# FFN activations read back later by ScalarE's queue in runs of 32, and state-space products in alternating heads: a two-layer decoder trunk on one Trainium2 core

## The chip, the cores and the metric

The kernel runs on one core of a Trainium2 chip. Five engines work on their own instruction queues: TensorE (PE in the profile, with its weight loads shown apart as PEld), VectorE (DVE), ScalarE (ACT), GpSimd (POOL) and SyncE (SP). A queue is worked off in order, and an instruction that waits for a semaphore holds what stands behind it. SP computes nothing here; it issues the DMAs. The metric is the device time of one execution in microseconds; the median of several runs is compared.

## What is computed

The reference takes 256 tokens of width 2048 through two layers. Cut to what matters here:

```python
for layer in range(2):
    hm = rms_norm(x, g) * (1 + sc_m) + sh_m          # sh, sc, g from the vector c
    y = ab_mixer(hm) if layer == 0 else cd_mixer(hm) # layer 0: gating MLP and a state-space scan
    x = x + (1 + g_m) * y
    hf = rms_norm(x, g) * (1 + sc_f) + sh_f
    x = x + (1 + g_f) * swiglu(hf, w_gate, w_up, w_down)

def swiglu(h, w_gate, w_up, w_down):                 # 2048 -> 5632 -> 2048
    a = silu(h @ w_gate) * (h @ w_up)
    return a @ w_down

def ssd_scan(x, dt, a, b_mat, c_mat):                # 32 heads of 64, chunks of 128 tokens
    ...
    y_diag = einsum('bcgrts,bcsgrp->bctgrp', cb[:, :, :, None] * decay, xc)
    ...
    y_off = einsum('bctgn,bcgrpn,bcgrt->bctgrp', cc, prev, exp(a_cum))
    return y_diag + y_off
```

Everything is float32.

## The kernel before

**Dense products.** A float32 product is made of three products of rounded parts (hi by hi, hi by lo, lo by hi). Weights stream from memory in slabs of two K tiles (128 rows each) by 512 columns. For each slab `wslab` (L322) issues the load on SP (L326, tile `raw`, 4 buffers), a cast on ScalarE (L332, `hi`, 3 buffers) and a rest on VectorE (L337, `lo`, 3 buffers). `dense_as` (L432) then runs the slab's 24 products of 128x512, four column by row groups of three for each tile, through `mm` (L156), with the activations as the stationary operand; `dense_ws` (L384) is the other way around and its products stand at L407. A dense product over 16 K tiles takes 8 slabs. After each slab `dense_as` calls `run_later`, which starts deferred work once DEFER = 6 K tiles of the running product are done, and `pump`, which paces the loads and sums of the modulation weights (`araw`, L234 and L201) beside the dense work.

**Order.** The kernel is written as one list; a planner orders each engine's queue by priority, by what depends on what, and by its own estimate of durations. `tc.high_priority(offset)` moves work ahead; `tc.issue_after` forces one instruction behind another. A deferred piece of work gets the priority of the place where it is called, so a later call means a later priority.

**FFN.** It runs in halves: 6 blocks of 512 columns, then 5, each block a gate product and an up product, and after each half the down product over its 24 or 20 tiles. The first half of layer 0 goes over K in two groups of 8 tiles (`grouped`, L585), with partial sums parked in buffers and put back as a seed (L615). The down product needs the activations transposed (features on partitions), as hi and lo parts. TensorE isn't used for that. `ffn_split` (L1354) calls `turned_by_blocks` (L499) on the block `sg` (silu of gate times up, evicted at L1375 or L1408):

- VectorE transposes 32x32 pieces into a tile `t` (L503, two instructions for each block).
- SP writes `t` to memory as the tensor `flip` with four DMAs (L507).
- A deferred `read` brings it back into `sg`'s own buffer with one DMA of 512 KB on SP (L513, forced behind the latest weight load). It is called when 6 tiles of the next product are done.
- A deferred `use` splits it: ScalarE makes hi (L523), VectorE lo (L524), both over 1024 elements a partition whose source elements lie eight apart. It is called after 10 tiles, or at the end of a product of 8.

This hand-over happens 22 times, 11 in each layer. Tiles of 4 KB a partition come from a pool of 14 buffers (`blk`).

**State-space products.** In layer 0, `ssd_group` (L957) works through four groups of 8 heads, in pairs. For each of the 16 pairs it builds decay masks `m` and `ce` on ScalarE and VectorE, then makes six products into one PSUM tile, head 0 in partitions 0 to 63 (the array's columns 0 to 63), head 1 in 64 to 127. Each is a full float32 product and stands in the trace as two records of 128x128 on 128*64 of the array. They are placed between the slabs of the dense products that run at the time.

Of the kernel before, what the change touches and what calls it, by code (L numbers as in the profile page):

```python
# [15 lines left out]
P = 128  # L16
S = 256
D = 2048
KT = D // P
# [25 lines left out]
F_RATES = (0.8, 0.62)  # L45
R_F1 = 0.5
DEFER = 6
ORDER = ("x4", "v0", "x5", "v1", "x0", "v2", "x1", "v3", "x2", "z0", "x3", "z1", "z2", "z3")
LN_AT = 9
GM_AT = (9, 11, 13, 15)  # L50
# [4 lines left out]
def trunk(ctx: ExitStack, tc: tile.TileContext, x, c, norm_mix_g, norm_ffn_g, ada_w, ada_b,  # L55
# [3 lines left out]
    nc = tc.nc  # L59
    V, A, G, T = nc.vector, nc.scalar, nc.gpsimd, nc.tensor  # L60
# [30 lines left out]
    def pm():  # L91
        return psM.tile([P, 512], F32, tag="m", name="pm")
# [62 lines left out]
    def mm(o, a, b, first=True, last=True):  # L155
        return T.matmul(o, a, b, start=first, stop=last, skip_group_check=True)  # L156
# [114 lines left out]
    wlast = [None, None]  # L271
# [76 lines left out]
    later = deque()  # L348
    dense_mm = [None]
    behind = [None]  # L350

    def run_later(done):
        while later and done >= (later[0][0] if isinstance(later[0], tuple) else 0):
            f = later.popleft()
            (f[1] if isinstance(f, tuple) else f)()

    preps = deque()

# [25 lines left out]
    def dense_ws(w, c0, ks, ahead=W_AHEAD, into=None, seeded=False, begun=None, ends=None):  # L384

        acc = (into or acc_tile()).rearrange("p (n t) -> p n t", n=4)
        done = 0
        for run in slabs(ks):  # L390
            run_prep()
            hi, lo = wslab(w, run[0][0], len(run), c0, 512, ahead)
            if ends and run[-1] is ks[-1]:
                ends()
            ops = []
            for i, (_, (bh, bl)) in enumerate(run):
                done += 1
                ops += [(hi[:, i, :], bh, done == 1, False), (hi[:, i, :], bl, False, False),
                        (lo[:, i, :], bh, False, done == len(ks))]
            if done <= 2:  # L400
                order = [(n, o) for i in (0, 2, 1) for n in range(4) for o in ops[i:i + 1]] \
                    + [(n, o) for n in range(4) for o in ops[3:]]
            else:
                order = [(n, o) for i in range(0, len(ops), 3) for n in range(4) for o in ops[i:i + 3]]
            for n, (a, b, first, final) in order:
                with (tc.issue_after(turned_sums[0].ins) if ends and done == len(ks) else ExitStack()):
                    dense_mm[0] = T.matmul(acc[:, n, :], a[:, n * P:(n + 1) * P], b,  # L407
                                           start=first and n % 2 == 0 and not seeded, stop=final, skip_group_check=True)
                if done == len(ks):
                    ends = None  # L410
            if begun and done == len(run):
                begun()
            if done >= min(DEFER, len(ks)):
                run_later(done if done < len(ks) else KT)
            pump()
        return acc

# [14 lines left out]
    def dense_as(w, c0, ks, ahead=W_AHEAD, head=None, tail=False, hold=False, into=None, seeded=False,  # L432
                 begun=None):

        if tail:
            accs = [pm(), pm()]
        else:
            full = (into or acc_tile()).rearrange("p (n t) -> p n t", n=2)  # L440
            accs = [full[:, 0, :], full[:, 1, :]]
        runs = list(slabs(ks))
        parts = [runs[:2]] if head else []
        end = len(runs) - 3 * tail
        parts += [[r] for r in runs[2 * len(parts):end]] + ([runs[end:]] if tail else [])
        done = 0
        for pi, part in enumerate(parts):
            begin = head and pi == 0
            made = []
            for j, run in enumerate(part):  # L450
                if not begin:
                    run_prep()
                made.append((run, *(ready.popleft() if ready else wslab(w, run[0][0], len(run), c0, 512, ahead))))
            done += sum(len(run) for run in part)
            ops = [(r, i, x) for r in range(len(part)) for x in range(3) for i in range(len(part[r]))]
            if begin:
                ops = [(r, i, x) for xs in ((0, 2), (1,)) for r in range(len(part)) for i in range(len(part[r]))
                       for x in xs]
            if len(part) > 1:
                order = [(n, j, o) for n in range(2) for j, o in enumerate(ops)]  # L460
            else:
                order = [(n, j, o) for j, o in enumerate(ops) for n in range(2)]
            for n, j, (r, i, x) in order:
                if begin and (n, j) in ((0, 0), (0, len(ops) - 2)):
                    head(int(j > 0))
                if begin and n == 1 and j == 8:
                    run_prep()
                run, hi, lo = made[r]
                bh, bl = run[i][1]() if callable(run[i][1]) else run[i][1]

                def product(n=n, j=j, i=i, x=x, bh=bh, bl=bl, hi=hi, lo=lo, last=pi == len(parts) - 1):
                    return mm(accs[n], (bl if x == 1 else bh)[:, n * P:(n + 1) * P], (lo if x == 2 else hi)[:, i, :],
                              first=pi == 0 and j == 0 and not seeded, last=last and j == len(ops) - 1)

                if hold and len(part) > 1 and n == 1 and j >= len(ops) - 2:
                    held.append(product)
                    continue
                with (tc.issue_after(dense_mm[0].ins) if len(part) > 1 and n == 1 and j == 0 else ExitStack()):
                    dense_mm[0] = product()
            if begun and pi == 0:  # L480
                begun()
            if done >= min(DEFER, len(ks)):
                run_later(done if done < len(ks) else KT)
            for _ in part:
                if not (tail and done > len(ks) - 16):
                    pump()
        return accs if tail else full
# [11 lines left out]
    def turned_by_blocks(src):  # L499

        t = bt()
        for cc in range(2):
            V.transpose(t.rearrange("p (c j f k) -> p k f c j", c=4, f=4, k=2)[:, cc],  # L503
                        src[:, cc, :].rearrange("p (f c j) -> p f c j", f=4, c=4))
        d = dram.tile([4, 32, 4, S], F32, tag="flip", name="flip", bufs=3)
        for q in range(4):
            nc.sync.dma_start(d[:, :, q, :].rearrange("c i x -> i c x"),  # L507
                              t[32 * q:32 * q + 32, :].rearrange("i (c x) -> i c x", c=4))
        back = src.rearrange("p c n -> p (c n)")

        def read():
            with tc.issue_after(wlast[0].ins):
                nc.sync.dma_start(back, d.rearrange("c i q x -> (c i) (q x)"))  # L513

        later.append(read)
        return back.rearrange("p (t m) -> p m t", m=8)

    def hslot(k):
        return (hp.tile([P, S], F32R, tag="h%d" % k, name="h%d" % k),
# [2 lines left out]
    def split(dst, src):  # L522
        A.activation(dst[0], src, AF.Copy)  # L523
        V.tensor_tensor(dst[1], src, dst[0].bitcast(F32), op=OP.subtract)  # L524
# [141 lines left out]
    with tc.high_priority(offset=50000):  # L666
# [25 lines left out]
        for k in range(0, KT, 2):  # L692
            ps = pm()
            for j in range(2):
                for cc in range(2):
                    src = xtok[2 * cc + (k + j) // 8][:, ((k + j) % 8) * P:((k + j) % 8 + 1) * P]
                    o = j * S + cc * P
                    last = mm(ps[:, o:o + P], src, diag[:, cc * P:(cc + 1) * P], first=(j == 0 and cc == 0))
# [258 lines left out]
    def ssd_group(g):  # L957
# [11 lines left out]
        xc = []  # L969
# [17 lines left out]
        for j in range(4):  # L987
# [14 lines left out]
            decay(kt + 2)  # L1002
            V.tensor_tensor(cev, cev, cT[:, None, P:S].to_broadcast([P, 2, P]), op=OP.mult)
            py = pm()
            for i in range(2):
                o = py[i * 64:(i + 1) * 64]
                es = slice((2 * j + i) * 64, (2 * j + i + 1) * 64)
                mm(o[:, 0:P], xc[0][:, es], m[:, i * S:i * S + P])
                mm(o[:, P:S], xc[1][:, es], m[:, i * S + P:(i + 1) * S], first=False, last=False)
                mm(o[:, P:S], sta[:, es], ce[:, i * P:(i + 1) * P], first=False)  # L1010
            V.scalar_tensor_tensor(xtile(kt), xtile(kt), dcol[:, kt:kt + 1], py[:, 0:S], op0=OP.mult, op1=OP.add)

    sums = st([P, 2, 4], "sums")
# [340 lines left out]
    def ffn_split(sg, f, a):  # L1354
        back, made = turned_by_blocks(sg), []

        def use():
            made.extend([b4(F32R), b4(F32R)])
            split([t.rearrange("p n (c t) -> p (n c) t", c=2) for t in made], back)

        later.append((DEFER + 4, use))
        for n in range(4):
            a.append((f + n, lambda n=n: [t[:, n, :] for t in made]))

# [246 lines left out]
```

## Time and profile before

| | |
|---|---|
| median of 3 runs | 2549.71 us (2549.46 to 2554.17) |
| the profiled execution | 2552.85 us, its span 2551.1 us |
| granted TensorE clock, mean | 0.998 |
| chain that ended last, by engine | PE 88%, DMA 5%, DVE 3%, ACT 2% |
| DMA queue of SP | 696.93 MB, 81.2% of the 16 engines' span |
| DMA queue of ScalarE | two small loads at the start |

The page gives for each engine its busy time and count of instructions, and for groups of like instructions the line in the kernel, the engine, what is written from what, the shape and count, then the busy time and mean duration, then the idle time of the engine just before them and who ended it. TensorE's matmuls are pipelined: the record of one 128x512 product lasts 0.39 us, but in a full stream one starts every 0.23 us, so lost time is read from how many start in a stretch, not from the busy share. A row of the table of stretches has the stretch, its length, the busy time and count of the engine asked for, the granted clock, the share of the DMA engines and GB/s. A row of the timeline has the start, the duration, engine, line, operation, tiles, shape and count, and in brackets the idle time before and its releaser.

### The profile page before, as it was taken

To read this page: it belongs to the slowest core of one execution; us is meant where nothing else is said; L and a number is where in the kernel's file an instruction comes from. 1 tells how busy PE (TensorE), PEld (TensorE's weight loads), DVE (VectorE), ACT (ScalarE), POOL (GpSimd) and SP (SyncE) were. 2 spreads that over 40 slices of the span, in tenths; PEclk is the share of its full clock that TensorE was granted. 3 is DMA by queue.
4 is the path that set the end of the run, shared out by engine and by line. 5 is a ranking of instruction groups with operands and counts; after the bars stand their busy time and mean duration, and the time that the engine had idled before them with its cause. 6 is when DMAs were issued, how large, how long until landed. Compare 5 with 4: busy or idle time off the path is not lost.

```text
span 2551.1 us, 33276 instructions
## 1 busy us (share of the span) xinstructions
PE 2512.1 (98%) x12293; PEld 2105.1 (83%) x12293; DVE 1881.4 (74%) x1983; ACT 1329.0 (52%) x1670; POOL 5.0 (0%) x19
## 2 busy tenths in 40 slices
PE   7999999999999999999999999999999999999999
PEld 6989898878788778888888788888788888888887
DVE  7888888899778788777888777667775555555554
ACT  5566876455645554334444665545744444344443
POOL 0000000000000000000000000000000000000000
PEclk9999999999999999999999999999999999999999
DMA  9998668989799899998999688888686776666665
GB/s 339 320 357 312 195 213 274 312 306 305 257 328 335 302 335 364 321 312 318 339 333 324 216 292 256 272 262 278 200 286 221 223 222 206 202 210 212 218 221 166
DMA packets 325533, 699.07 MB, mean 274 GB/s; under 512 B 26096, under 2 KB 39930, under 8 KB 325370
## 3 DMA queue, kind: packets, MB, share of 16 engines
q1 hardware_dynamic: 325242, 696.93, 81.2%
q8 instruction: 96, 1.57, 0.2%
q14 instruction: 67, 0.55, 0.1%
q10 hardware_dynamic: 128, 0.02, 0.0%
HBM read 683.15 MB, written 13.70 MB: 273 GB/s over the span
## 4 chain that ended last, share of the span: by engine, by line
PE 88%; DMA 5%; DVE 3%; ACT 2%; issue 2%; SPq 1%; DVEq 0%; ACTq 0%
PE accps L156 73%; PE accps L407 8%; PE pm L156 6%; DMA blk<-flip 1%; DMA flip<-blk 1%; PE pm L153 1%; DVE acc L201 1%; DVE lo L337 1%; ACT blk L523 1%; ACT hi L332 1%; DMA raw<-in_ffn_w_gate 0%; SPq L507 0%; DMA blk<-in_ada_w 0%; DVE blk L503 0%; DMA raw<-in_ffn_w_down 0%
## 5 line engine op out<-in xcount | busy, mean ns | idle before, releaser
L332 ACT ACTIVATE hi<-raw 128x1024 fp32r<-128x1024 f32 (+1 forms) x864 | 898.5, 1045 | 1032.2 <-PE accps L156 816.5
L337 DVE TENSOR_TENSOR lo<-raw,hi 128x1024 fp32r<-128x1024 f32 (+1 forms) x864 | 1035.7, 1206 | 467.2 <-ACT hi L332 460.5
L156 PE MATMUL accps<-hi,h 128*128 128x512 f32 x2224 | 603.8, 392 | 6.3 <-ACT hi L332 6.3
L156 PE MATMUL accps<-lo,h 128*128 128x512 f32 x2224 | 602.2, 392 | 1.4 <-DVE lo L337 1.2
L156 PE MATMUL accps<-hi,l 128*128 128x512 f32 x2224 | 601.4, 391 | 0.0
L156 PEld LDWEIGHTS accps<-lo,h 128*128 128x128 f32 x2224 | 415.8, 188 | 92.0 <-DVE lo L337 5.7
L156 PEld LDWEIGHTS accps<-hi,l 128*128 128x128 f32 x2224 | 417.3, 188 | 87.6 <-issue 0.8
L156 PEld LDWEIGHTS accps<-hi,h 128*128 128x128 f32 x2224 | 413.1, 188 | 92.6 <-ACT hi L332 8.9
L201 DVE SCALAR_TENSOR_TENSOR acc<-araw,ct,acc 128x1024 f32<-128x1024 f32 (+2 forms) x377 | 465.6, 1235 | 4.2 <-DMA araw<-in_ada_w 3.4
L156 PE MATMUL accps<-hi,blk 128*128 128x512 f32 x1440 | 357.2, 390 | 0.0
L156 PEld LDWEIGHTS accps<-hi,blk 128*128 128x128 f32 x1440 | 269.7, 188 | 56.2 <-ACT hi L332 0.3
L156 PE MATMUL accps<-lo,blk 128*128 128x512 f32 x720 | 192.9, 390 | 1.0 <-DVE lo L337 1.0
L407 PE MATMUL accps<-h,hi 128*128 128x256 f32 x624 | 163.3, 285 | 2.2 <-ACT hi L332 1.4
L407 PE MATMUL accps<-h,lo 128*128 128x256 f32 x624 | 164.4, 287 | 0.9 <-DVE lo L337 0.9
L407 PE MATMUL accps<-l,hi 128*128 128x256 f32 x624 | 162.5, 285 | 1.2 <-DVE l L567 1.2
L156 PEld LDWEIGHTS accps<-lo,blk 128*128 128x128 f32 x720 | 135.0, 188 | 29.7 <-DVE lo L337 1.8
L407 PEld LDWEIGHTS accps<-h,hi 128*128 128x128 f32 x624 | 114.4, 192 | 4.3 <-ACT hi L332 1.6
L407 PEld LDWEIGHTS accps<-h,lo 128*128 128x128 f32 x624 | 114.1, 193 | 2.7 <-DVE lo L337 1.7
L407 PEld LDWEIGHTS accps<-l,hi 128*128 128x128 f32 x624 | 114.2, 193 | 1.6 <-DVE l L567 1.4
L524 DVE TENSOR_TENSOR blk<-blk 128x1024 fp32r<-128x1024 f32 x22 | 47.7, 2168 | 79.2 <-ACT blk L523 79.2
L523 ACT ACTIVATE blk<-blk 128x1024 fp32r<-128x1024 f32 x22 | 47.4, 2157 | 73.1 <-DMA blk<-flip 72.9
L156 PE MATMUL pm<-hi,blk 128*128 128x512 f32 x224 | 57.1, 391 | 0.0
(281 smaller groups left out, 1361.3 us busy)
## 6 DMA issues: line engine op xcount, KB each, us to landing
araw<-in_ada_w SPq DMA_DIRECT2D x323, 512.0 KB, 5.7
raw<-in_ffn_w_gate SPq DMA_DIRECT2D x176, 512.0 KB, 4.9
raw<-in_ffn_w_up SPq DMA_DIRECT2D x176, 512.0 KB, 5.1
raw<-in_ffn_w_down SPq DMA_DIRECT2D x176, 512.0 KB, 4.8
raw<-in_ab_w_in SPq DMA_DIRECT2D x128, 512.0 KB, 4.9
raw<-in_cd_w_in SPq DMA_DIRECT2D x96, 512.0 KB, 4.6
raw<-in_ab_w_out SPq DMA_DIRECT2D x64, 512.0 KB, 5.5
raw<-in_cd_w_out SPq DMA_DIRECT2D x32, 512.0 KB, 5.1
```

Source lines behind the costliest of these rows:

```text
L153: return T.transpose(dst, src, ident)
L156: return T.matmul(o, a, b, start=first, stop=last, skip_group_check=True)
L201: V.scalar_tensor_tensor(acc, r, ct[nr][:, g:g + 1], acc, op0=OP.mult, op1=OP.add)
L332: A.activation(hi, raw, AF.Copy)
L337: wlast[1] = V.tensor_tensor(lo, raw, hi.bitcast(F32), op=OP.subtract)
L407: dense_mm[0] = T.matmul(acc[:, n, :], a[:, n * P:(n + 1) * P], b, start=first and n % 2 == 0 and not seeded, stop=final, skip_group_check ...
L523: A.activation(dst[0], src, AF.Copy)
L524: V.tensor_tensor(dst[1], src, dst[0].bitcast(F32), op=OP.subtract)
```

## The change

Three edits. In the hand-over, the transposes write another layout, in which the 32 elements that one split instruction reads in turn lie side by side; the read-back is issued by ScalarE's queue and no longer forced behind a weight load; the read is called 10 K tiles after the hand-over and the split 14, counted over all dense products in `run_later` by a running count, no longer within the next product. In the state-space products the two heads of a pair alternate.

```diff
+FLIP_READ = 10
+FLIP_SPLIT = 14
...
-    def run_later(done):
-        while later and done >= (later[0][0] if isinstance(later[0], tuple) else 0):
-            f = later.popleft()
-            (f[1] if isinstance(f, tuple) else f)()
+    timed = []
+    ktiles = [0]
+
+    def after_tiles(n, f):
+        timed.append((ktiles[0] + n, len(timed), f))
+        timed.sort(key=lambda e: e[:2])
+
+    def run_later(now, n):
+        ktiles[0] += n
+        while timed and timed[0][0] <= ktiles[0]:
+            timed.pop(0)[2]()
+        while later and now:
+            later.popleft()()
...
-            if done >= min(DEFER, len(ks)):
-                run_later(done if done < len(ks) else KT)
+            run_later(done >= min(DEFER, len(ks)), len(run))
...
-            V.transpose(t.rearrange("p (c j f k) -> p k f c j", c=4, f=4, k=2)[:, cc],
+            V.transpose(t.rearrange("p (c f k j) -> p k f c j", c=4, f=4, k=2)[:, cc],
                         src[:, cc, :].rearrange("p (f c j) -> p f c j", f=4, c=4))
...
-        def read():
-            with tc.issue_after(wlast[0].ins):
-                nc.sync.dma_start(back, d.rearrange("c i q x -> (c i) (q x)"))
-
-        later.append(read)
-        return back.rearrange("p (t m) -> p m t", m=8)
+        after_tiles(FLIP_READ, lambda: nc.scalar.dma_start(back, d.rearrange("c i q x -> (c i) (q x)")))
+        return back.rearrange("p (q m i) -> p m q i", q=4, i=32)
...
+            os = [py[i * 64:(i + 1) * 64] for i in range(2)]
+            es = [slice((2 * j + i) * 64, (2 * j + i + 1) * 64) for i in range(2)]
             for i in range(2):
-                o = py[i * 64:(i + 1) * 64]
-                es = slice((2 * j + i) * 64, (2 * j + i + 1) * 64)
-                mm(o[:, 0:P], xc[0][:, es], m[:, i * S:i * S + P])
-                mm(o[:, P:S], xc[1][:, es], m[:, i * S + P:(i + 1) * S], first=False, last=False)
-                mm(o[:, P:S], sta[:, es], ce[:, i * P:(i + 1) * P], first=False)
+                mm(os[i][:, 0:P], xc[0][:, es[i]], m[:, i * S:i * S + P])
+            for i in range(2):
+                mm(os[i][:, P:S], xc[1][:, es[i]], m[:, i * S + P:(i + 1) * S], first=False, last=False)
+            for i in range(2):
+                mm(os[i][:, P:S], sta[:, es[i]], ce[:, i * P:(i + 1) * P], first=False)
...
-            split([t.rearrange("p n (c t) -> p (n c) t", c=2) for t in made], back)
-
-        later.append((DEFER + 4, use))
+            split([t.rearrange("p n (c q i) -> p (n c) q i", c=2, q=4) for t in made], back)
+
+        after_tiles(FLIP_SPLIT, use)
```

`dense_ws` calls `run_later` in the same new way. The layout of `flip` in memory and the four writes on SP stay as they were.

More of the change, by code (lines that the diff above doesn't have):

```diff
@@ L481, in dense_as @@
                 begun()
-            if done >= min(DEFER, len(ks)):
-                run_later(done if done < len(ks) else KT)
+            run_later(done >= min(DEFER, len(ks)), sum(len(run) for run in part))
             for _ in part:
```

## The prediction

> **What bounds the kernel now.** I read the page first (busy time, then the costliest groups), next a table of stretches, then the waits, and last the timeline around two hand-overs of the turned FFN activations.
>
> ```profile
> PE 2512.1 (98%) x12293; PEld 2105.1 (83%) x12293; DVE 1881.4 (74%) x1983; ACT 1329.0 (52%) x1670; POOL 5.0 (0%) x19
> ...
> L332 ACT ACTIVATE hi<-raw 128x1024 fp32r<-128x1024 f32 (+1 forms) x864 | 898.5, 1045 | 1032.2 <-PE accps L156 816.5
> L337 DVE TENSOR_TENSOR lo<-raw,hi 128x1024 fp32r<-128x1024 f32 (+1 forms) x864 | 1035.7, 1206 | 467.2 <-ACT hi L332 460.5
> ...
> L524 DVE TENSOR_TENSOR blk<-blk 128x1024 fp32r<-128x1024 f32 x22 | 47.7, 2168 | 79.2 <-ACT blk L523 79.2
> L523 ACT ACTIVATE blk<-blk 128x1024 fp32r<-128x1024 f32 x22 | 47.4, 2157 | 73.1 <-DMA blk<-flip 72.9
> ```
>
> TensorE is the bound: 98% busy. ScalarE's weight casts (L332) wait for TensorE to free a buffer, 816.5 us in all, so they are early. What is not TensorE's own pace can only be won in small holes. The 22 splits of turned activations (L523, L524) take twice the time of a weight cast or rest of the same 1024 elements, 2157 against 1045 ns and 2168 against 1206, and ScalarE stands 72.9 us waiting for their data. How many of these microseconds reach TensorE, the stretches tell.
>
> ```profile
> 1010.00:1130.00 120.00, 120.00 (x531) 1.00 0.94 326
> 840.00:960.00 120.00, 115.04 (x498) 0.99 0.94 320
> 1150.00:1160.00 10.00, 8.98 (x38) 1.00 0.72 254
> 1240.00:1250.00 10.00, 9.26 (x39) 1.00 0.70 248
> ```
>
> An undisturbed stretch of 120 us holds 531 products, so one takes 0.226 us. The second K group of layer 0's first FFN half (840 to 960) holds 33 fewer: 33 x 0.226 = **7.5 us** lost. Ten undisturbed microseconds hold 44.2; 1150 to 1160 and 1240 to 1250 miss 6.2 and 5.2: **2.6 us** at two hand-overs of the later half. For layer 1 I take the waits, between 1860 and 2460 us for the weight load, and over the whole run for the DMA queue:
>
> ```profile
> PEld accps L156 <- DVE lo L337: 2.8, 5, 0.7
> ```
>
> ```profile
> SPq L513 <- DMA flip<-blk: 70.6, 38, 4.4
> ```
>
> So layer 1 loses at most **2.8 us**, and SP, which issues every weight load, stands 70.6 us in front of the read-back (L513) until the flip's writes have landed. What that does is seen at the second hand-over, first on SP, then on the engines:
>
> ```profile
> 872.55 0.39 SPq L326 DMA_DIRECT2D raw<-in_ffn_w_gate  x1
> 877.18 0.34 SPq L513 DMA_DIRECT2D blk<-flip  x1
> 877.57 0.43 SPq L326 DMA_DIRECT2D raw<-in_ffn_w_gate  x1
> ```
>
> ```profile
> 882.89 2.04 ACT L523 ACTIVATE blk<-blk 128x1024 fp32r<-128x1024 f32 x1 [5.04 <-DMA blk<-flip]
> 884.84 1.99 ACT L332 ACTIVATE hi<-raw 128x1024 fp32r<-128x1024 f32 x2
> 884.96 2.08 DVE L524 TENSOR_TENSOR blk<-blk 128x1024 fp32r<-128x1024 f32 x1 [5.86 <-ACT blk L523]
> 885.93 0.19 PEld L156 LDWEIGHTS accps<-hi,h 128*128 128x128 f32 x1 [3.51 <-ACT hi L332]
> ```
>
> SP issues nothing from 872.94 to 877.18: 4.2 us. The read lands 5.7 us after its issue, ScalarE stands 5.04 us before the split and works 2.04 on it, and two casts follow only at 884.84. TensorE's weight load has by then waited 3.51 us. In layer 1 the same pattern is milder:
>
> ```profile
> 2268.27 1.06 ACT L332 ACTIVATE hi<-raw 128x1024 fp32r<-128x1024 f32 x1 [1.66 <-PE accps L156]
> 2270.99 1.06 ACT L332 ACTIVATE hi<-raw 128x1024 fp32r<-128x1024 f32 x1 [1.66 <-PE accps L156]
> 2276.45 2.15 ACT L523 ACTIVATE blk<-blk 128x1024 fp32r<-128x1024 f32 x1 [4.40 <-DMA blk<-flip]
> 2278.51 1.05 ACT L332 ACTIVATE hi<-raw 128x1024 fp32r<-128x1024 f32 x1
> ```
>
> ```profile
> 2280.72 4.63 DVE L337 TENSOR_TENSOR lo<-raw,hi 128x1024 fp32r<-128x1024 f32 x4
> 2280.76 1.07 PE L156 MATMUL accps<-hi,l 128*128 128x512 f32 x4
> 2282.00 0.77 PEld L156 LDWEIGHTS accps<-lo,h 128*128 128x128 f32 x4 [0.59 <-DVE lo L337]
> ```
>
> Casts come every 2.72 us (2268.27, 2270.99), one for each slab of two K tiles; with three buffers a cast serves a slab three later, so ScalarE may be late by 3 x 2.72 - 1.06 = 7.1 us. The cast due at 2273.71 starts at 2278.51, 4.8 late, inside that. But VectorE's rests start behind its own 2.17 us split and miss TensorE by 0.59 us.
>
> **The change part by part. Split (14 tiles, runs of 32).** The elements now lie 32 side by side, no longer eight apart, which is the layout of the weight cast. ScalarE's split falls from 2.16 to about 1.05 us, VectorE's from 2.17 to 1.21. That is 2.1 us sooner for the rests behind them; layer 1's holes are 0.7 us or less. The transposes that write this layout:
>
> ```profile
> L503 DVE STREAM_TRANSPOSE blk<-blk 128x512 f32<-128x512 f32 x44 | 47.4, 1159 | 0.0
> ```
>
> No row shows one writing runs of 32. From 1159 (nothing won) down to half of it, 0.58 us, by the ratio 2157 to 1045; I take 0.6, because the strided write is their only oddity. The flip's writes then leave about 1.1 us earlier. All this is ScalarE and VectorE time beside TensorE, worth only what the holes hold.
>
> **Read-back on ScalarE's queue (10 tiles).** SP loses 22 issues of 0.34 us and 70.6 us of standing; the weight loads behind it go out on time. ScalarE gains 22 issues, for which there is one row:
>
> ```profile
> 0.80 0.98 ACTq L113 DMA_DIRECT2D t<-in_c  x2
> ```
>
> 0.49 us each, 10.8 us together, hidden because the casts are early (above); without that cover it would be 10.8 us. ScalarE also gains the wait for the flip's writes. Behind it on that engine stand the weight casts, then SiLU and the seeding copies; VectorE's rests and TensorE wait for those casts. Ten tiles are 5 x 2.72 = 13.6 us after a product ends. In layer 1 the eviction of the product begins at 2261.02 and SP saw the writes landed at 2272.81, 11.8 us later, 10.7 with faster transposes: a read standing at its own position waits for nothing. The planner may put it earlier, as it did the old split, which stands before the cast of 2273.71 though written after 10 tiles. Between nothing and SP's 4.4 us, I take 2 to 3 us: one cast late, inside the 7.1. The read still lands 3.6 (layer 1) to 5.7 us after issue; the split follows two slabs, 5.4 us, later. Its wait shrinks from 4.4 to at most 2 us, and what is late next is nothing that TensorE asks for.
>
> So: layer 1 wins **2.0** of 2.8; the later half of layer 0 **2.4** of 2.6. Of the 7.5 us in 840 to 960 I take **4.5**: the transfers there run at 320 GB/s with a share of 0.94, against 326 in the undisturbed stretch, so part of the hole is the DMA engines' own limit and stays. The bounds are 0 and 7.5. The last block of each five-block half is needed by TensorE at tile 16 of the down projection, one slab (2.72 us) after the split's position; the split takes 1.05 + 1.21 = 2.3. Were it late, that costs up to 3 us at two places; I put it at nothing and leave it to the range. Buffers: the turned tile lives four tiles longer, the split's pair is taken four tiles later, and the next hand-over is 16 tiles off.
>
> The DMA page speaks against the queue change. The Trainium skill, "DMA: Bandwidth & Descriptors", section "Issuing engines are not separate DMA queues", says that DMAs from scalar, sync and gpsimd share the same 16 engines and that issuing on several saves only the sequencer's time to initiate. By that alone SP would be spared 22 x 0.34 us, all hidden, and the three terms would be nothing (first rival). The rows of SP show what it does not count: 70.6 us in which the issuing sequencer stands and the weight loads behind it aren't issued.
>
> **State-space products.** Each pair of heads makes six products, each two records. The records of a head fill one half of the array's columns (128*64).
>
> ```profile
> 367.86:368.87 1.01, 1.01 (x9) 1.00 0.65 156
> ...
> 564.58:565.16 0.58, 0.58 (x5) 1.00 0.90 307
> 566.05:568.16 2.11, 2.11 (x29) 1.00 1.02 310
> 572.71:573.78 1.07, 1.07 (x13) 1.00 0.95 314
> sum 17.22, PE 17.22; mean PE 1.15
> ```
>
> ```profile
> 374.80 0.27 PE L156 MATMUL pm<-t,sta 128*64 128x128 f32 x1
> 374.86 0.27 PE L156 MATMUL pm<-t,xc 128*64 128x128 f32 x1
> 374.91 0.27 PE L156 MATMUL pm<-t,sta 128*64 128x128 f32 x1
> 374.97 0.27 PE L156 MATMUL pm<-t,xc 128*64 128x128 f32 x1
> ```
>
> These are fifteen runs, first and last with the sum (each count holds one record of what follows). Eight records of one half in 1.01 us and four in 0.58: 0.108 us each and 0.15 for entering and leaving the mode. Where records of both halves alternate, as at 374.80, one starts every 0.056 us: two run at once. Today they overlap only in the middle of a run, since a head's three products come first; a run of twelve takes 1.07. Fully paired it takes 0.15 + 12 x 0.054 = 0.80, and all 192 take 15 x 0.15 + 192 x 0.054 = 12.6 instead of 17.2: **4.6 us** at best, nothing at worst. VectorE is the next limit there:
>
> ```profile
> 515.00:580.00 65.00, 65.00 (x340) 51.38 (x339) 61.84 (x77) 36.49 (x69) 3.45 (x6) 1.00 0.87 298
> ```
>
> 61.84 of 65 us busy; half of the saving falls into this stretch, which could shrink to 62.7 and VectorE would be full. I take **3.5**.
>
> **Sum:** 3.5 + 2.0 + 2.4 + 4.5 = 12.4 us. The profiled execution took 2552.85 us (its span is 2551.1, 1.75 lie around it) and would take 2540.4; it stands 3.1 over the median 2549.71, from which I get **2537**.
>
> **Rivals.** (1) *The wait only changes its queue* (the page's rule): ScalarE stands where SP stood, and the casts come as late as today. For it: the read cannot start before the writes land. Against it: the weight loads are freed and the split is halved. The flip terms are nothing, 2549.7 - 3.5 = 2546. Chance 0.17. (2) *The pairing gives nothing*, because VectorE or a planner's new order takes it back: 2549.7 - 8.9 = 2541. For it, 61.84 of 65; against it, the 0.056. Chance 0.15. (3) *Slower:* no cast stands between read and split in ScalarE's queue. At the second hand-over it would stand 4.2 us for the writes, 0.5 issuing, 5.7 for the read, 1.05 on the split: 11.5. The cast due 2.72 us into that is 8.8 late, 1.7 over the 7.1; with the rest's 1.2 behind it up to 2.9. Eleven such hand-overs in layer 0 are 19 to 32 us, in place of the 10.1 lost today, less 5.5 won elsewhere: +4 to +16, about 2560. It decides from 7.1 us of lateness on; one cast between (5.8 + 5.7 standing, the next cast 6 late) avoids it. Chance 0.10, since the two are written two slabs apart.
>
> **How the numbers follow.** Forecast 0.58. The range reaches from all bounds won (4.6 + 2.8 + 2.6 + 7.5 = 17.5: 2532, and 3 for a shifted order) to rival 1 with both late splits and some noise: 2529 to 2551; outside are rival 3 and a tail, under 0.2. A change of 0.2% is 5.1 us, about what a measurement can tell from none. Faster: 0.58, rival 2's 0.13 and a little of rival 1: 0.74. Same: 0.16. Slower: 0.10.
>
> **What would show it.** Right: no SP wait at the read; splits of about 1.05 and 1.21 us; transposes near 0.6; about 525 products or more in 840 to 960; the fifteen runs near 12.6 us in sum, a lone run of twelve at 0.8. Wrong: weight loads of TensorE waiting for casts behind an ACT wait on the flip's writes; VectorE filling the state-space stretch; 0.108 between records there.

## The result, and the profile after

The changed kernel takes 2538.58 us (median of 4 runs, 2536.96 to 2539.53), the kernel before beside it 2549.59: a ratio of 0.9947, with an interval of 0.9935 to 0.996. The profiled execution took 2539.53 us, its span is 2537.8. It is faster by 11 us; 2537 was predicted. The sum came out; one of its largest terms had the wrong cause, as the experiments show.

The page of the changed kernel, then one row of its table of groups and two of its DMA issues (name, queue, count, KB each, median us from issue to landing):

```profile
PE 2502.1 (99%) x12293; PEld 2097.3 (83%) x12293; DVE 1843.9 (73%) x1983; ACT 1302.9 (51%) x1670; POOL 5.0 (0%) x19
...
L528 DVE TENSOR_TENSOR blk<-blk 128x1024 fp32r<-128x1024 f32 x22 | 26.9, 1224 | 48.3 <-ACT blk L527 48.3
L527 ACT ACTIVATE blk<-blk 128x1024 fp32r<-128x1024 f32 x22 | 23.3, 1059 | 68.2 <-DMA blk<-flip 68.2
```

```profile
L512 DVE STREAM_TRANSPOSE blk<-blk 128x512 f32<-128x512 f32 x44 | 28.6, 688 | 0.0
```

```profile
flip<-blk SPq DMA_DIRECT2D x88, 128.0 KB, 4.4
blk<-flip ACTq DMA_DIRECT2D x22, 512.0 KB, 5.1
```

Each operation became as cheap as foreseen: splits of 1.06 and 1.22 us, transposes of 0.69 in place of 1.16. But ScalarE still stands 68.2 us in front of the split, against 72.9 before. The waits of ScalarE and of SP's queue:

```profile
ACT blk L527 <- DMA blk<-flip: 68.2, 20, 5.1
ACT hi L334 <- DMA flip<-blk: 20.2, 6, 5.1
```

```profile
SPq L328 <- DMA flip<-blk: 4.0, 5, 1.2
```

SP's 70.6 us in front of the read are gone, and ScalarE has taken over at least 20.2 of them. The stretches of the prediction (time, PE, PEld, DVE, ACT and POOL busy with counts, clock, DMA share, GB/s):

```profile
840.00:960.00 120.00, 116.30 (x512) 94.00 (x510) 94.26 (x90) 59.67 (x61) 0.00 (x0) 1.00 0.94 334
1150.00:1160.00 10.00, 10.00 (x45) 8.27 (x45) 9.22 (x8) 3.65 (x4) 0.00 (x0) 1.00 1.02 382
1240.00:1250.00 10.00, 10.00 (x45) 8.26 (x45) 7.72 (x8) 4.25 (x4) 0.00 (x0) 1.00 1.01 377
```

The two hand-overs of layer 0's later half have no hole any more. The second K group holds 512 products, against 498 before and 531 undisturbed: 19 are still lost, 4.3 us. (A second profile of the same kernel, c_after_again below, has 525 there.) Rows of the second hand-over, from three views of the engines:

```profile
862.85 2.94 ACT L334 ACTIVATE hi<-raw 128x1024 fp32r<-128x1024 f32 x3
...
872.21 0.33 ACTq L519 DMA_DIRECT2D blk<-flip  x1
872.91 1.06 ACT L334 ACTIVATE hi<-raw 128x1024 fp32r<-128x1024 f32 x1 [7.12 <-PE accps L158]
874.02 0.76 PEld L158 LDWEIGHTS accps<-hi,h 128*128 128x128 f32 x4 [1.57 <-ACT hi L334]
...
878.98 1.06 ACT L527 ACTIVATE blk<-blk 128x1024 fp32r<-128x1024 f32 x1 [2.06 <-DMA blk<-flip]
881.04 0.77 PEld L158 LDWEIGHTS accps<-hi,h 128*128 128x128 f32 x4 [1.46 <-ACT hi L334]
```

```profile
869.99 0.54 SPq L236 DMA_DIRECT2D araw<-in_ada_w  x1
875.25 0.37 SPq L328 DMA_DIRECT2D raw<-in_ffn_w_gate  x1
```

ScalarE ends three casts at 865.79 and then stands until the read leaves at 872.21; the cast behind it starts at 872.91 and TensorE's weight load has waited 1.57 us for it. (The view puts the 7.12 us down to a product, the last of several releasers. The order of the queue shows that the read, which waits for the flip's writes, stood ahead.) ScalarE stands again before the split, and TensorE waits another 1.46 us. SP isn't free either: between 870.53 and 875.25 it issues nothing. Its waits between 866 and 890 us:

```profile
SPq L328 <- DVE lo L339: 11.7, 5, 4.6
```

A load of weights needs a buffer that the rest (L339) of an earlier slab has read, and the rest follows the late cast.

### The profile page after: what moved, and what is told of

Its sections match the earlier page's. It is cut to its first block, busy times and chain, and to the rows that moved or that the text cites. A ratio compares the mean times of both kernels' runs of the same rounds, so it can differ in the third digit from the quotient of the medians.

```text
span 2537.8 us, 33322 instructions
## 1 busy us (share of the span) xinstructions
PE 2502.1 (99%) x12293; PEld 2097.3 (83%) x12293; DVE 1843.9 (73%) x1983; ACT 1302.9 (51%) x1670; POOL 5.0 (0%) x19
## 3 DMA queue, kind: packets, MB, share of 16 engines
q8 instruction: 96, 1.57, 0.2%
## 4 chain that ended last, share of the span: by engine, by line
PE 90%; DMA 4%; DVE 3%; ACT 2%; issue 1%; SPq 0%; DVEq 0%; ACTq 0%
PE accps L158 76%; PE accps L418 7%; PE pm L158 6%; DVE acc L203 1%; PE pm L155 1%; DMA blk<-flip 1%; DMA raw<-in_ffn_w_down 1%; DMA flip<-blk 1%; DVE lo L339 1%; ACT hi L334 0%; DMA araw<-in_ada_w 0%; DMA blk<-in_ada_w 0%; DVE t L957 0%; ACT t L1031 0%; DMA raw<-in_ffn_w_gate 0%
## 5 line engine op out<-in xcount | busy, mean ns | idle before, releaser
L339 DVE TENSOR_TENSOR lo<-raw,hi 128x1024 fp32r<-128x1024 f32 (+1 forms) x864 | 1034.8, 1204 | 518.8 <-ACT hi L334 513.3
L418 PEld LDWEIGHTS accps<-h,hi 128*128 128x128 f32 x624 | 113.9, 191 | 4.0 <-ACT hi L334 1.6
L418 PEld LDWEIGHTS accps<-h,lo 128*128 128x128 f32 x624 | 113.3, 191 | 3.4 <-DVE lo L339 2.3
L418 PEld LDWEIGHTS accps<-l,hi 128*128 128x128 f32 x624 | 113.3, 191 | 1.9 <-DVE l L571 1.4
L528 DVE TENSOR_TENSOR blk<-blk 128x1024 fp32r<-128x1024 f32 x22 | 26.9, 1224 | 48.3 <-ACT blk L527 48.3
L527 ACT ACTIVATE blk<-blk 128x1024 fp32r<-128x1024 f32 x22 | 23.3, 1059 | 68.2 <-DMA blk<-flip 68.2
```

The costliest lines, as they stand in the source:

```text
L339: wlast[1] = V.tensor_tensor(lo, raw, hi.bitcast(F32), op=OP.subtract)
```

## The experiments

In this table the stand of ScalarE is the sum of its waits for the flip's writes and for the read, and of its 22 splits. Waits that the view puts down to another releaser, like the 7.12 us above, are missing from it. Like the second group it is read from the one profiled execution, and not from the median beside it. The second group is the time from the first transposes of hand-over 1 to those of hand-over 6, both in layer 0, in each profile; the same kernel gave 120.4 and 117.9, and 113.3 and 112.2, so differences under 3 us say little.

| kernel | layout, read's queue, heads | median us | ratio, interval | ScalarE, us | second group, us |
|---|---|---|---|---|---|
| before | old, SP, apart | 2549.59 | 1 | 72.9 + 47.4 = 120 | 123.5 |
| e1_pairs_only | old, SP, alternating | 2550.37 | 0.9991, 0.9982 to 1.0 | 73.4 + 47.4 = 121 | 122.4 |
| e8_fast_transpose | transposes new, SP, apart | 2544.9 | 0.997, 0.9961 to 0.998 | 60.1 + 47.5 = 108 | 118.2 |
| e9_fast_split | split new, SP, apart | 2542.97 | 0.9961, 0.9949 to 0.9973 | 72.3 + 23.3 = 96 | 117.3 |
| e3_layout_only | new, SP, apart | 2539.16 | 0.9944, 0.9932 to 0.9957 | 63.6 + 23.3 = 87 | 114.0 |
| e4_old_layout | old, ScalarE, alternating | 2564.26 | 1.0046, 1.0034 to 1.0058 | 47.7 + 59.4 + 47.4 = 155 | 127.8 |
| e2_handover_only | new, ScalarE, apart | 2540.41 | 0.9954, 0.9941 to 0.9966 | 24.9 + 65.8 + 23.3 = 114 | 119.6 |
| after | new, ScalarE, alternating | 2538.58 | 0.9947, 0.9935 to 0.996 | 20.2 + 68.2 + 23.3 = 112 | 120.4 |
| c_after_again | the same | 2540.35 | 0.9949, 0.9937 to 0.9962 | 26.1 + 67.2 + 23.3 = 117 | 117.9 |
| e7_pool_queue | new, GpSimd, alternating | 2540.81 | 0.9957, 0.9944 to 0.997 | 85.7 + 23.3 = 109 | 117.6 |
| e10_later_read | new, ScalarE later, alternating | 2533.78 | 0.993, 0.9918 to 0.9943 | 10.6 + 47.7 + 23.3 = 82 | 113.9 |
| e5_sync_queue | new, SP, alternating | 2535.15 | 0.9927, 0.9915 to 0.994 | 59.7 + 23.3 = 83 | 113.3 |
| e5_again | the same | 2534.94 | 0.9933, 0.9919 to 0.9946 | 59.7 + 23.3 = 83 | 112.2 |

The ratios are each to the kernel before on the same chip, whose median lay between 2549.59 and 2553.35.

**The heads alone, and the hand-over alone.** e1 takes only the alternating products into the kernel before; e2 is the changed kernel with them put back:

```
...
             for i in range(2):
...
-                mm(o[:, 0:P], xc[0][:, es], m[:, i * S:i * S + P])
-                mm(o[:, P:S], xc[1][:, es], m[:, i * S + P:(i + 1) * S], first=False, last=False)
-                mm(o[:, P:S], sta[:, es], ce[:, i * P:(i + 1) * P], first=False)
+                mm(os[i][:, 0:P], xc[0][:, es[i]], m[:, i * S:i * S + P])
+            for i in range(2):
+                mm(os[i][:, P:S], xc[1][:, es[i]], m[:, i * S + P:(i + 1) * S], first=False, last=False)
+            for i in range(2):
+                mm(os[i][:, P:S], sta[:, es[i]], ce[:, i * P:(i + 1) * P], first=False)
```

> The kernel before with the alternating heads alone; the hand-over is untouched. Theory (the two edits are independent and TensorE takes the whole of what the pairing frees): the fifteen or so runs of state-space records cost about 13.0 us in sum in place of 17.2, and the kernel is 4.2 us shorter, ratio 0.9984. Rival (VectorE, 61.84 of 65 us busy there, takes it back): the runs cost 13.0 but the first hand-over starts less than 2 us earlier than before and the ratio is over 0.9992.

> The changed kernel with the heads of a pair one after the other again. Theory (independent edits): the hand-overs bring 9 us of span whatever comes before them: 3 in the second K group of layer 0, 3 in layer 0's later half, 2.5 in layer 1; ratio 0.9965. Rival (the hand-over's gain is partly a shift of the plan by the earlier state-space work): under 6 us and another share by stage.

e2 gives 0.9954, a larger gain than the 0.9965 of its theory; by stage its profile shows 3.9, 2.5 and 1.8 us, for the 3, 3 and 2.5 foreseen. e1 gives 0.9991, between the two theories, with an interval that reaches 0.2% of gain and none. Together they make 0.55%, the whole change 0.51 to 0.53%: the two edits add up as far as the runs can tell. The profiled execution of e1, 2544.33 us, is the fastest of its 11, and that of e2, 2545.94 us, the slowest of its 5, so their stages stand for one execution and not for the median. The state-space records themselves are plain. Three of the 17 stretches of the changed kernel that hold all 192, first, a lone run of twelve and last, and the sum of all 17:

```profile
367.05:368.07 1.02, 1.02 (x17) 1.00 0.63 173
...
563.06:563.87 0.81, 0.81 (x14) 1.00 0.88 341
567.94:568.75 0.81, 0.81 (x14) 1.00 0.97 283
sum 13.05, PE 13.05; mean PE 0.77
```

They took 17.2 us and take 13.05. A run of twelve takes 0.81 (the counts include neighbours), as foreseen. In wall time the medians give 2.5 us (before to e1), 1.8 (e2 to after, on two chips) and 4.0 (e3 to e5_sync_queue, which also differ in where the read and the split are called).

**The layout alone.** e3 is the kernel before with only the three views changed, the read on SP at its old place:

```
-            V.transpose(t.rearrange("p (c j f k) -> p k f c j", c=4, f=4, k=2)[:, cc],
+            V.transpose(t.rearrange("p (c f k j) -> p k f c j", c=4, f=4, k=2)[:, cc],
...
-        return back.rearrange("p (t m) -> p m t", m=8)
+        return back.rearrange("p (q m i) -> p m q i", q=4, i=32)
...
-            split([t.rearrange("p n (c t) -> p (n c) t", c=2) for t in made], back)
+            split([t.rearrange("p n (c q i) -> p (n c) q i", c=2, q=4) for t in made], back)
```

> The kernel before with the runs of 32 alone (transposes, split); the read stays on SP, forced behind a weight load and called at 6 tiles. Theory (the split and the rests behind it were layer 1's and the later half's holes, the queue was the hole of the second K group): layer 1 wins its 2.4 us, the later half of layer 0 most of its 3, the second K group 1 or less because SP still stands 3 to 4 us before the read; ratio 0.9978, about 5.5 us. Rival (the queue is what counts): under 2 us in all, TensorE still waits for rests and casts at the layer 1 hand-overs.

Both theories missed. The layout alone brings 0.56%, some 14 us, as much as the whole change, with the order of instructions on TensorE, ScalarE, SP and GpSimd unchanged. Its second K group, and its SP queue:

```profile
840.00:960.00 120.00, 119.90 (x534) 98.97 (x533) 100.74 (x96) 63.25 (x63) 0.00 (x0) 1.00 0.98 349
```

```profile
SPq L513 <- DMA flip<-blk: 69.8, 42, 5.2
```

SP stands in front of the read as long as before, 69.8 against 70.6 us, and TensorE loses nothing in that group. So SP's standing alone doesn't make the hole, nor does the DMA engines' rate: they now move 349 GB/s there.

**Which half of the layout.** e8 has only the new transposes, e9 only the new split (the first pair of lines of the diff above, or the other two). Each alone hands the features to the down product in another order, so these two don't compute the reference; the instructions and their order on every engine are those of the kernel before.

> The kernel before with the new transposes (runs of 32 written side by side) and the old strided split, so that the features meet the down product in another order. Theory S (the split's 1.1 us less on ScalarE and 0.95 less on VectorE, right ahead of weight casts, are the gain): the transposes alone are worth little, ratio 0.998 to 1.0. Theory W (the transposes, 0.45 us each and ahead of the writes, let writes, read and split all come earlier): ratio 0.9945 to 0.996.

> The kernel before with the old strided transposes and the new split over runs of 32, the features again in another order. Theory S: nearly all of the layout's gain, ratio 0.9945 to 0.996, with the transposes still at 1.16 us and the splits at 1.06 and 1.22. Theory W: ratio 0.998 to 1.0.

Both halves count, and neither theory was right alone: 0.997 and 0.9961. Their second groups, e8 and e9:

```profile
840.00:960.00 120.00, 118.03 (x520) 96.04 (x519) 100.91 (x92) 66.43 (x61) 0.00 (x0) 1.00 0.95 338
```

```profile
840.00:960.00 120.00, 118.94 (x524) 96.67 (x523) 101.44 (x92) 61.59 (x62) 0.00 (x0) 1.00 0.97 339
```

498 products became 520 with the transposes, 524 with the split, 534 with both. Two transposes before the writes are 0.94 us shorter (2 x (1159 - 688)), the split 1.1 on ScalarE: about 2 us of one serial chain, transposes, writes, read, split, then the cast for which TensorE waits. At the second hand-over this chain, from the start of the transposes to the start of the cast behind the split, takes 17.9 us before, 16.3 in e8, 17.2 in e9 and 15.5 in e3.

**The read's queue alone.** e5 is the changed kernel with the read issued by SP; on ScalarE nothing else moves, and the orders of TensorE and VectorE stay the same:

```
-        after_tiles(FLIP_READ, lambda: nc.scalar.dma_start(back, d.rearrange("c i q x -> (c i) (q x)")))
+        after_tiles(FLIP_READ, lambda: nc.sync.dma_start(back, d.rearrange("c i q x -> (c i) (q x)")))
```

> The changed kernel with the read issued by SP again, called at 10 tiles. Theory (queue pays in the second K group only): SP stands before the read again (about 70 us over 22), ScalarE no longer waits for the flip's writes; 1 to 3 us longer than the changed kernel, all of it between the first hand-over and the end of the first half of layer 0; ratio to before 0.996. Rival 1 (the queue is what counts): 6 us or more longer than the changed kernel. Rival 2 (ScalarE's standing before the read costs as much as SP's did): no longer than the changed kernel.

0.9927, beyond rival 2: the queue is a loss, not a gain. (The intervals just overlap, but all ten runs of e5 and e5_again, 2532.98 to 2536.46 us, lie below all nine of the changed kernel, 2536.96 to 2540.89.) Its second hand-over and its read:

```profile
868.62 1.06 ACT L334 ACTIVATE hi<-raw 128x1024 fp32r<-128x1024 f32 x1 [1.97 <-DMA raw<-in_ffn_w_up]
...
871.31 0.34 SPq L519 DMA_DIRECT2D blk<-flip  x1
871.59 1.04 ACT L334 ACTIVATE hi<-raw 128x1024 fp32r<-128x1024 f32 x1
875.41 1.06 ACT L527 ACTIVATE blk<-blk 128x1024 fp32r<-128x1024 f32 x1 [2.78 <-DMA blk<-flip]
876.38 1.99 ACT L334 ACTIVATE hi<-raw 128x1024 fp32r<-128x1024 f32 x2
```

```profile
blk<-flip SPq DMA_DIRECT2D x22, 512.0 KB, 3.8
```

(These rows are of its second run, e5_again.) The casts of 868.62 and 871.59 run while the writes land; in the changed kernel they start at 872.91 and 875.88. The read also lands 3.8 us after its issue, against 5.1.

**The queue with the old layout.** e4 is the changed kernel with the minus lines of e3's diff. It ran beside the changed kernel itself.

> The changed kernel itself, beside the next three on one chip. Both theories: ratio 0.9947 to the kernel before (0.9935 to 0.996 earlier), about 2539 us.

> The changed kernel with the old strided layout of the turned activations (transposes and split as before), the read on ScalarE's queue, heads alternating. Theory now (the layout is the gain, ScalarE's queue is a loss of 4 to 5 us, the heads are worth 2 to 4): the loss and the heads cancel, ratio 0.999 to 1.001, and TensorE loses at least as much in the second K group (840 to 960 us) as in the kernel before. Rival, as predicted (freeing SP's queue fills that group): 4.5 us of the group and the heads' 2 to 4 stay without the layout, ratio 0.9965 to 0.9975.

Slower than the kernel before, 1.0046, worse than either theory. The second group and the waits of ScalarE:

```profile
840.00:960.00 120.00, 113.22 (x484) 89.77 (x483) 96.90 (x86) 61.69 (x58) 0.00 (x0) 0.99 0.90 310
```

```profile
ACT blk L527 <- DMA blk<-flip: 59.4, 20, 4.2
ACT hi L334 <- DMA flip<-blk: 44.2, 12, 4.2
ACT blk L1411 <- DMA flip<-blk: 3.5, 1, 3.5
```

With e1, e5 and the changed kernel this makes a square, all with alternating heads. Its fourth corner, e1, also calls the read at 6 tiles and the split at 10, where the other three have 10 and 14; what that alone does with the old layout wasn't tried. With this reserve, moving the read to ScalarE costs 0.55% (about 14 us) with the old layout; with the new one, where nothing else differs, it costs 0.16 to 0.2% (4 to 5 us). The layout gives 0.6% with the read on SP (0.56% in e3, where nothing else differs) and 1% with it on ScalarE. With the longer chain more casts stand behind the read: 12 waited for the flip's writes, 44.2 us in all, against 6 and 20.2 in the changed kernel.

**Why ScalarE's queue costs.** e7 issues the read from GpSimd, which has almost nothing to do:

```
-        after_tiles(FLIP_READ, lambda: nc.scalar.dma_start(back, d.rearrange("c i q x -> (c i) (q x)")))
+        after_tiles(FLIP_READ, lambda: nc.gpsimd.dma_start(back, d.rearrange("c i q x -> (c i) (q x)")))
```

e10 leaves it on ScalarE, but behind the latest weight cast:

```
-FLIP_READ = 10
-FLIP_SPLIT = 14
+FLIP_READ = 14
+FLIP_SPLIT = 16
...
-                A.activation(hi, raw, AF.Copy)
+                wlast[2] = A.activation(hi, raw, AF.Copy)
...
-        after_tiles(FLIP_READ, lambda: nc.scalar.dma_start(back, d.rearrange("c i q x -> (c i) (q x)")))
+        def read():
+            with tc.issue_after(wlast[2].ins):
+                nc.scalar.dma_start(back, d.rearrange("c i q x -> (c i) (q x)"))
+        after_tiles(FLIP_READ, read)
```

> The changed kernel with the read back issued by GpSimd, which is busy for 5 us of the span, in place of ScalarE. Theory Q1 (ScalarE stands at the read for the writes, with the weight casts queued behind it, and that is what the queue costs): no cast stands any longer, ratio 0.992 to 0.9935, about the time with the read on SP's queue (0.9927) or below it, and TensorE loses under 1.5 us in layer 0's gated network. Theory Q2 (a second queue beside SP's takes the DMA engines from the weights, or the read's packets come out later in it, whatever engine issues it): ratio 0.9945 to 0.9955, as with ScalarE.

> The changed kernel with the read still on ScalarE's queue, but placed behind the weight cast that is the latest then (at 14 K tiles, the split at 16), so that at the first two hand-overs and later ones one more cast stands ahead of the read. Theory Q1: ScalarE stands for less, and the cast behind it is needed a weight load later: between the changed kernel (0.9948) and the read on SP (0.9927), 0.9932 to 0.9943. Theory Q2: no change, 0.9944 to 0.9956. A third case: the split now lands later than its first product needs it, over 0.996.

> The changed kernel with the read issued by SP, as before, beside the other two on one chip. Both theories: ratio 0.9927 (0.9915 to 0.994 earlier), about 2534 us.

e10 gives 0.993, with Q1 and a little better than it expected. e7 gives 0.9957, with Q2 and a little worse than it expected. GpSimd's read in e7 (the wait for it, then its issues), and e10's:

```profile
ACT blk L527 <- DMA blk<-flip: 85.7, 18, 7.0
```

```profile
blk<-flip POOLq DMA_DIRECT2D x22, 512.0 KB, 6.1
```

```profile
ACT blk L528 <- DMA blk<-flip: 47.7, 20, 4.9
ACT hi L334 <- DMA flip<-blk: 5.4, 2, 3.1
ACT blk L1411 <- DMA flip<-blk: 5.2, 3, 2.3
```

```profile
blk<-flip ACTq DMA_DIRECT2D x22, 512.0 KB, 6.5
```

Each theory holds half. From a queue beside SP's the read lands later (4.8 to 6.5 us in the median over all runs, against 3.6 to 3.9 from SP's), as Q2 says; in e10 that costs nothing to be seen, though the read lands latest there. In e7 it goes with a long stand of ScalarE in front of the split, 85.7 us. The ScalarE column, whichever wait fills it, nearly orders the profiled executions from which it is read. With the heads apart 120, 114, 108, 96 and 87 us go with 2552.85, 2545.94, 2543.62, 2542.97 and 2539.98 us (before, e2, e8, e9, e3). With alternating heads 155 and 121 go with 2565.46 and 2544.33 (e4, e1), 109 to 117 with 2539.53 to 2540.89 and 82 to 83 with 2533.32 to 2535.21. The medians fit less well: e2's 0.9954 with 114 us lies below the ratios of e8 and e9, with 108 and 96. e7 and e10 change the planned order of some other instructions too. So this column goes with the time and is no price for each microsecond, and that ScalarE's stand is the whole of the queue's loss is argued, not shown; shown is the loss itself, in e5.

e5 and e10 beat both kernels, at about 2535 and 2534 us; their intervals don't tell them apart.

## Why the prediction was right, and where it was wrong

**The sum.** 12.4 us were predicted for the profiled execution, and its span shrank by 13.3. Up to hand-over 1 it gained 4.5, in the second K group 3.1, in the later half 3.0 and in layer 1 1.6; 1.1 lie elsewhere. That the total fits is in part luck, since in the largest term a gain of twice the size met a loss that wasn't foreseen.

**State-space pairing, 3.5: right, as far as the runs are sure.** The first state-space record starts at 367.86 us before and at 367.05 after, the first transposes of hand-over 1 at 841.64 and 837.11: between them the changed kernel gains 4.53 - 0.81 = 3.7 us. 4.2 of the records' time went (17.2 to 13.05). The medians give 1.8 to 4.0. One pair of profiles is not sure to a microsecond there: the start of hand-over 1 lies between 841.6 and 844.3 us in the five profiles with the heads apart and between 836.1 and 841.1 in the eight with alternating heads, 4.7 apart in the mean. VectorE, the rival's limit, did not take it back.

**Later half of layer 0, 2.4: right but for the queue, a little small.** From hand-over 7 to hand-over 11 it took 176.77 us and takes 173.79, a gain of 3.0. e3, e8 and e9 all come within 0.03 us of that time, so either half of the layout is enough there, and the queue adds nothing. With the old layout it takes 177.9 in e4 and 176.4 in e1.

**Layer 1, 2.0: the hole is gone, its size isn't settled.** TensorE's weight load waited 2.8 us for rests there. After, and in e1 with its old hand-over, between the same 1860 and 2460 us:

```profile
PEld accps L158 <- ACT hi L334: 0.3, 1, 0.3
```

```profile
PEld accps L156 <- DVE lo L337: 1.2, 3, 0.6
```

Part of the 2.8 belonged to that one execution. From hand-over 12 to hand-over 22 it took 568.5 us, e1 with the same hand-over took 567.7 and the changed kernel 567.0: a gain of 0.7 to 1.6. e3 has 566.8 with the read on SP.

**Second K group, 4.5: the step that failed.** The prediction gave the gain to "the weight loads behind it go out on time" and left the rest to "the DMA engines' own limit". The time gained there was 3.1 us, 5.6 in the second profile, so the size looked right. But it is the sum of two that weren't seen: the layout alone gains 9.5 us there (123.5 to 114.0, e3), and the queue gives back 5 to 8 (112.2 and 113.3 with SP, 117.9 and 120.4 with ScalarE). Nor was there a limit of the DMA engines to leave something for: e3 moves 349 GB/s there and loses no product. The shorter operations were priced in layer 1 and the later half alone. In the rows that the prediction quoted at the second hand-over, TensorE's weight load waited 3.51 us for a cast behind a split of 2.04 us, and that was the wait to price. SP's 4.2 us without an issue stood beside it and was taken for the cause. In e9, SP stands 3.9 us at the same place, and the group is 6.2 us shorter all the same. Two more rows of the kernel before, SP's waits between 866 and 890 us, point the same way:

```profile
SPq L326 <- DVE lo L337: 9.3, 4, 6.8
SPq L513 <- DMA flip<-blk: 4.1, 1, 4.1
```

SP waited longer for buffers, which the late casts and rests free, than for the writes.

**The wait on ScalarE, "2 to 3 us: one cast late, inside the 7.1": mis-sized, and so was the 7.1.** ScalarE stood 6.4 us for the read at the second hand-over, and TensorE waited for the cast behind it. TensorE's products there, in the changed kernel:

```profile
864.56 1.07 PE L158 MATMUL accps<-hi,h 128*128 128x512 f32 x4
865.46 1.07 PE L158 MATMUL accps<-hi,l 128*128 128x512 f32 x4
866.37 1.07 PE L158 MATMUL accps<-lo,h 128*128 128x512 f32 x4
...
871.81 1.07 PE L158 MATMUL accps<-lo,h 128*128 128x512 f32 x4
874.02 1.19 PE L158 MATMUL accps<-hi,h 128*128 128x512 f32 x4 [1.14 <-ACT hi L334]
```

A slab is 12 products, three groups of four (not the 24 named ahead of the prediction), and its `hi` is in use until the second group ends. So the buffer of the slab of 864.56 came free at 866.53, and the cast into it, for the slab three later, was due then. That slab would have begun at 872.72, the 0.91 us of a group behind 871.81, so the cast, 1.06 us long, could be 5.1 us late. It began at 872.91, 6.4 late: inside the predicted 7.1, and TensorE lost 1.3 us. The kernel before gives the same cover in layer 1, for the cast of 2268.27:

```profile
2266.26 1.07 PE L156 MATMUL accps<-hi,h 128*128 128x512 f32 x4
2267.16 1.07 PE L156 MATMUL accps<-hi,l 128*128 128x512 f32 x4
...
2274.42 1.07 PE L156 MATMUL accps<-hi,h 128*128 128x512 f32 x4
```

The buffer comes free at 2268.2, three slabs on is 2274.42, and 2274.42 - 2268.27 - 1.06 is 5.1. The prediction took three whole slabs, and left out the 2 us in which a slab still uses its `hi`. So rival 3 was decided from 5.1 us of lateness on, not from 7.1.

The split's wait was to shrink "from 4.4 to at most 2 us". It went from 72.9 to 68.2 us in all. The read was to land within two slabs, 5.4 us, ahead of the split. It lands 5.1 us after its issue in the median, where it took 3.6 before, and 6.8 at the second hand-over, where ScalarE, being late, was through with the two casts between after 4.7. The issue itself was cheaper than taken, 0.33 us.

**The rivals.** That the wait only changes its queue was true of the wait and wrong about the time, since the layout pays without it. The Trainium skill's rule ("DMA: Bandwidth & Descriptors", "Issuing engines are not separate DMA queues"), that issuing from another engine saves only the time to initiate, agrees with e7, e10 and e5: no other queue beat SP's beyond the intervals. The loss on the engine that then stands comes on top: 4 to 5 us from e5 to the changed kernel. The slower rival, ScalarE standing through both transfers with the casts behind it, happened with the old layout: 2564 us in e4, where the prediction had 2560. It needed no missing cast; two stand between read and split. The stand ahead of them, 6.89 us in e4's second hand-over, goes with it.

Of the signs named ahead: SP's wait at the read went, the splits, the transposes (0.69, not 0.6) and the run of twelve came as told, the records' sum at 13.05 and not 12.6. 512 products and not 525 were in 840 to 960 (525 in the second profile), and the weight load behind a ScalarE wait on the writes, named as a sign of a wrong reason, was there.

## What to carry to other kernels

When a wait is moved to another engine's queue, count what stands behind it there before counting what it frees: here the freed queue soon stood for the buffers that the late casts should have emptied. Take the cover of an early engine from the moment at which its buffer comes free in the trace, not from the number of buffers. In a serial chain between two engines, shorten the operations first (runs of 32 elements for elements eight apart halved the splits); that alone paid some 14 us. When two parts of a change meet at one hole, a right total says nothing of either; run them apart.

## What the runs showed of the hardware

- VectorE and ScalarE took 1.8 and 2.0 times as long on f32 elements eight apart as on runs of 32: 2168 against 1224 ns, and 2157 against 1059. The transposes, which write one or the other, took 1159 and 688. The Trainium skill ("Advanced Engine Details and Errata", "SBUF Cachelines") says that accesses which each hit another 16-byte line of SBUF are penalised; elements 32 bytes apart do, and the runs agree. The size here is a factor of 1.7 to 2.0.
- The same 512 KB read landed 3.6 to 3.9 us (medians of the runs) after its issue from SP's queue, and 4.8 to 6.5 from ScalarE's or GpSimd's. On SP it was issued after SP had stood with nothing else issued (4.2 us at the second hand-over before), while with another queue SP's loads of weights go out around it. That these slow it fits, but it was not tried by itself.
- A run of twelve records of 128x128 on 128*64 of the array took 1.07 us with the two halves of its columns in groups and 0.81 us with the halves alternating; all 192 took 17.2 and 13.05.
